# Index keys split two steps ahead, a deeper queue of selection rounds, value pages V3 before the cross pages, and a fourth raw weight buffer

## The chip, the cores and the metric

The kernel runs on one core of one Trainium2 chip. The metric is the time of one execution on the device, in microseconds (us). A core has TensorE (PE) for matmuls, with its weight loads shown apart as PEld, VectorE (DVE), ScalarE (ACT), GpSimd (POOL) and SyncE (SP), which here issues the transfers. Each engine works through its own list of instructions in order; where two engines share data, one waits for the other by a semaphore.

## The reference

One step of a decoder layer, for a prompt of 256 tokens and 8 sample requests with 8 new tokens each (320 token rows, `NT`), model width 2048. One projection of the residual stream feeds three branches: sparse attention (A) whose keys are chosen by an indexer, a gated linear recurrence (B), and cross-attention to a memory (M). Each branch is multiplied by a SiLU gate, the three are concatenated and go through an output projection and a layer norm.

```python
def _in_proj(h, w, pos):
    z = jnp.einsum('btd,dn->btn', h, w)
    aq, ak, av, ag, iq, ik, iw, bq, bf, bi, bg, mq, mg = jnp.split(z, cuts, axis=-1)
    ...
def _indexer_scores(iq, iw, ik):
    dots = jnp.einsum('bthd,bld->bthl', iq, ik) * (D_IDX ** -0.5)          # 16 heads x 64
    return jnp.einsum('bth,bthl->btl', iw * (H_IDX ** -0.5), relu(dots))
def _dsa_sample(q, k_new, v_new, iq, iw, ik_new, cache_k, cache_v, cache_idx_k, page_table):
    ik_all = concatenate([cache_idx_k[page_table], ik_new])                # 2048 + 8 keys a request
    sc = where(kpos <= qpos, _indexer_scores(iq, iw, ik_all), -inf)
    _, sel = lax.top_k(sc, 256)
    # attention of 8 heads x 128 over the 256 selected keys and values of the paged cache
    ...
def _merge(...):
    cat = concatenate([a * silu(ag), rmsnorm(b) * silu(bg), m * silu(mg)])  # 2048 wide
    return layernorm(ALPHA * h + cat @ w_out)
```

## The kernel before

**Precision.** All matmuls against weights are done in three products of a fast fp32 form (fp32r): each operand is split into a high part and a rest. For the residual stream these are `xh` and `xl`; for a weight half (128 x 512 of a raw weight tile `wr`, 128 x 1024) ACT casts `wh` from `wr` and DVE or POOL subtracts `wl = wr - wh`. There are three buffers of `wr` and four each of `wh` and `wl`. The first 52 weights have their `wl` on DVE; later ones go to DVE or POOL, whichever is free sooner by the planner's costs (`TT`). While the selection on the sample scores runs, `hold_dve` adds 4 us to DVE's side of that choice.

**Stages.** PE works through the list `PROJECTIONS`: index keys and queries, attention queries, keys and values, the recurrence's inputs, gates, then 16 weights of kind "mem" (the projection of the memory), then the rest and last the output projection `wo`. One 128-deep slice of a projection is three matmuls `pj<-xh,wh`, `pj<-xl,wh`, `pj<-xh,wl` of 320 columns. `xh` and `xl` are reused for the concatenated branches (`cat`) when the last projection has read them: process `split` casts `xh<-cat` on ACT and subtracts `xl` on POOL and DVE, and the first `wo` matmul (`mA<-wh,xh`) needs them.

**Pages.** Between projection slices PE makes visits to the cache pages, which SP loads into six buffers `pg`: keys (`kv<-pg,qpad`, 32 or 16 matmuls) and values (`va<-pg,PT`). `PAGES` is their order: K0 to K3 and V0 to V3 are pairs of heads of the paged cache, 8 units each, XK and XV the cross-attention cache.

**Indexer on the samples.** `idx_sample` has 20 steps, 16 of 512 keys and 4 of the 8 new keys. A step's keys are gathered, then split by `stack(k)`: ACT casts the high halves and DVE subtracts the two rests into the tile `cat1`, in one of two slots by the parity of the step (64x512 each, rows `cat<-pg,cat` and `cat<-S,cat` on DVE; in the order below the tile's name is `cat_4_84` before and `cat_5_83` after). Four matmuls `mA<-cat,bp` or `mB<-cat,bp` follow, then relu, and every few steps the sums over heads (`va<-cat,t`). `topk_sample` then takes 32 rounds of MAX8 and MATCH_REPLACE8 over the scores on DVE (tile `PT`). `idx_prompt` does the same for the prompt, in smaller rounds (tile `cat0`), and leaves its mask in `pbias`. `attn_scores` and `attn_values` are the prompt's attention, and `"attn" in done` marks their end.

**What sets the order.** The program is a planner: class `Plan` keeps a time for each engine from cost formulas, `plan.now` follows PE, and the loop at the end of the function emits loads (`loads`), weight splits (`prep`), evacuations of finished projections and pieces of the background processes (generators) whenever their conditions are met at the planned time. `need(...)` makes a process wait until its operands are planned to be ready, `idle("DVE", x)` until DVE's planned queue is at most x us, and `calm()` holds the recurrence's long rows back while an engine's queue is over `CALM` = 4 us. The result is a fixed list of instructions for every engine. All instructions that go through the planner's `Engine` carry one line of the profile, L154, so they are told apart by their tiles. `tabm` is the rope table of the attention heads, `lbt` the lower bounds of the recurrence.

Of the kernel before, what the change touches and what calls it, by code (L numbers as in the profile page):

```python
# [26 lines left out]
NS, NT = 64, 320  # L27
PAST = 2048
HALF = 1032
PROJECTIONS = ["ikw", "iq", "aq", "ak", "av", "b0", "b1", "g0", "b2", "g1", "b3", "mem", "mq", "g3", "g2"]  # L30
PAGES = ["K0", "K1", "V0", "K2", "V1", "V2", "K3", "XK0", "XK1", "XV0", "XV1", "V3"]
DEFER = (0,)
MIX = [(1, 2), (1, 4), (1, 6), (2, 0)]
KORDER = (0, 2, 4, 6, 12, 14, 8, 10)
# [10 lines left out]
CALM = 4.0  # L45
# [180 lines left out]
def hymba_step(ctx: ExitStack, tc: tile.TileContext, I, O):  # L226
    nc = tc.nc
    plan = Plan()
# [39 lines left out]
    def const(shape, name, dt=F32):  # L268
        return pool.tile(shape, dt, name=name, tag=name, bufs=1)
# [42 lines left out]
    xh = const([128, 16, NT], "xh", F32R)  # L312
    xl = const([128, 16, NT], "xl", F32R)
    ident = const([128, 128], "ident")
    tabm = const([128, 2, NT], "tabm")
    csm = const([128, 297], "csm")
    cu8 = const([128, 304], "cu8", U8)
    ptab = const([1, 128], "ptab", I32)
# [7 lines left out]
    one = const([128, 1], "one")  # L326
    onesm = const([128, 128], "onesm")
    emat = const([128, 2, 2, 2, 128], "emat", BF)
    pbias = const([128, 384], "pbias")
    maskb = const([128, HALF], "maskb", BF)  # L330
    early, stacked = new([128, 2880], "cat0"), new([128, 2240], "cat1", F32R)
    plan.split |= {early.tensor.name, stacked.tensor.name}
# [13 lines left out]
    done = set()  # L346
# [232 lines left out]

    WR, WH, WL = {}, {}, {}  # L580

    def load_w(i):
        s = wspec[i]
        WR[i] = s["home"] if "home" in s else new([128, 1024], "wr")
        SP.dma_start(WR[i][:, 0:s["n"]], s["src"])
        if s["kind"] == "mem":
            s["raw"] = T(256)
            SP.dma_start(s["raw"], I["memT"][:, s["k"], :])
# [259 lines left out]
    def idx_sample():  # L848
# [67 lines left out]

        while not keys_in(0):
            yield
        kk = stack(0)
        rs, full = {}, None  # L920
        for k, (sp, c, f, a) in enumerate(steps):
            n = kk[0].shape[-1]
            yield need(ql, qh, *kk, ps=2, lag=LAG2)
            pd = [PS([128, 512]), PS([128, 512])]
            for j in range(2):
                b = 4 * sp + 2 * a + j
                PE.matmul(pd[j][:, 0:n], qh[:, b], kk[j], start=True, stop=False)
                PE.matmul(pd[j][:, 0:n], qlr[:, b], kk[j], start=False, stop=True)
            if full:
                sums(*full)  # L930
                full = None
            r = rs.setdefault((c, f), [])
            for j in range(2):
                r.append(relu_slot(n))
                if j == 0 or plan.t["ACT"] < plan.t["DVE"] + 0.5:
                    ACT.activation(r[-1], pd[j][:, 0:n], AF.Relu)
                else:
                    DVE.tensor_scalar(r[-1], pd[j][:, 0:n], 0.0, None, op0=OP.max)
            if a == 1 and (c, f) in ((0, 0), (2, 1)):
                full, rs = (sp, rs), {}  # L940
            while not keys_in(k + 1):
                yield
            if k + 1 < len(steps):
                kk = stack(k + 1)
                yield
        yield need(*[x for r in full[1].values() for x in r], ps=1)
        sums(*full)
# [6 lines left out]
    def topk_sample(sc, arena):  # L954
        w1 = arena[:, HALF:2 * HALF]
        L = arena[:, 2 * HALF:2 * HALF + 256]
        for r in range(32):
            yield from idle("DVE", 0.3)
            m8 = L[:, 8 * r:8 * r + 8]
            src = sc if r == 0 else w1  # L960
            DVE.max(m8, src)
            DVE.match_replace(out=w1, in_to_replace=m8, in_values=src, imm_value=FLOOR)
# [283 lines left out]

    def calm():

        while max(plan.t[e] for e in ("DVE", "POOL", "ACT")) > plan.now + CALM:
            yield  # L1250

    def hgrn():
# [648 lines left out]
    def loads():  # L1901
        nonlocal nw, npg
        while True:
            if plan.t["SP"] > plan.now + 0.5:
                return
            if nw < len(wspec) and wspec[nw].get("ref"):
                nw += 1
                continue
            if nw < len(wspec) and nw < half + 5 and plan.slot_free("wr", 3) <= plan.now + 1 and nw - nprep < 3 \
                    and (wspec[nw]["kind"] != "mem" or has_room(3)):  # L1910
                load_w(nw)
                nw += 1
                continue
            if outq and plan.avail(outq[0][1]) <= plan.now:
                dst, src = outq.pop(0)
                SP.dma_start(dst, src)
                free(src)
                continue
            if later_in and plan.t["DMA"] < plan.now + IDLE:
                dst, src = later_in.pop(0)  # L1920
                SP.dma_start(dst, src)
                continue
            n, b = divmod(npg, 2)
            if (half > 46 and n < len(punits) and len(PG) + ("q" in st) + ("more" in st) + ci_live(0) < BUFS["pg"] and n <= nunit + 2
                    and plan.slot_free("pg", BUFS["pg"]) <= plan.now + 0.2 and plan.t["DMA"] < plan.now + 8):
                load_pages(n, b)
                npg += 1
                continue
            if ("soft", 3) in done and half > n_in - 6 and ("r", 1) not in st:
                ln_load(0)  # L1930
                ln_load(1)
                continue
            if n == len(punits) and nunit == n and half > n_in - 6 and ("r", 2) not in st:
                ln_load(2)
                continue
            return
# [177 lines left out]
```

## Time and profile before

| | |
|---|---|
| median of 3 runs | 877.13 us (876.77 to 878.39) |
| profiled execution, own time | 878.17 us |
| its span | 876.4 us |
| granted TensorE clock | 0.998 |
| PE, DVE, ACT, POOL busy | 860.5, 558.0, 423.0, 311.7 us |
| last matmul starts | 868.17 us |
| moved by DMA | 266.55 MB, 304 GB/s in the mean |

The profile is of one execution. Times within it run from the start of the span; the runs' times also hold what lies around the span. "Idle before" in a row is the time for which the engine did nothing ahead of it, with what ended the wait. The ends of matmuls are modelled: a 320-column matmul shows 0.31 us, while the next one starts 0.15 us later.

### The profile page before, as it was taken

Reading aid. Unit: us, or ns where it says so; the run is one execution under the profiler, and the core shown is the slowest. Engines: PE = TensorE matmul, PEld = TensorE weight load, DVE = VectorE, ACT = ScalarE, POOL = GpSimd, SP = SyncE. Lnnn points to the kernel's source line nnn. Section 1 sums busy time; section 2 is a strip of 40 time slices with the busy share of each in tenths; the row PEclk is TensorE's granted clock in tenths of the full one; section 3 lists DMA queues with packets and bytes.
Section 4 is the critical chain, followed back from the end, with each engine's and each line's share of the span. In section 5 each row is a group of like instructions: output and inputs, shape, how many; then the busy total and the mean of one; then the engine's idle time right before and its main releaser. Section 6 shows DMA issues by size and latency. Waiting matters only on the chain.

```text
span 876.4 us, 19974 instructions
## 1 busy us (share of the span) xinstructions
PE 860.5 (98%) x6972; PEld 730.7 (83%) x6974; DVE 558.0 (64%) x1128; ACT 423.0 (48%) x909; POOL 311.7 (36%) x310
## 2 busy tenths in 40 slices
PE   9999999999999999999999999999999999999996
PEld 8999898878988998879888786777888878788885
DVE  6778989748789984645745563585444333943655
ACT  6445666545463444435545364444444433744432
POOL 0543562255644461322433142334222000613424
PEclk9999999999999999999999999999999999999999
DMA  8555544899999975999999999999998999876633
GB/s 309 182 165 160 158 144 146 300 342 405 362 410 337 372 260 161 339 411 354 398 367 399 412 377 401 405 347 383 325 408 331 350 384 384 295 269 200 192 101 120
DMA packets 84375, 266.55 MB, mean 304 GB/s; under 512 B 10609, under 2 KB 21810, under 8 KB 83634
## 3 DMA queue, kind: packets, MB, share of 16 engines
q1 hardware_dynamic: 83250, 263.18, 81.3%
q0 software_dynamic: 1024, 2.10, 0.8%
q8 instruction: 55, 0.90, 0.4%
q14 instruction: 46, 0.38, 0.1%
HBM read 256.50 MB, written 8.73 MB: 303 GB/s over the span
## 4 chain that ended last, share of the span: by engine, by line
PE 91%; DMA 3%; DVE 2%; ACT 1%; SPq 1%; issue 1%; DVEq 0%; ACTq 0%
PE pj L154 53%; PE mB L154 11%; PE va L154 10%; PE mA L154 9%; PE kv L154 7%; DMA pg<-in_ck 2%; SPq L154 1%; ACT wh L154 1%; DVE wl L154 1%; DMA pg<-in_xT 1%; DVE t L154 1%; DMA wr<-in_wt 0%; DVE pg L154 0%; ACT t L154 0%; DVE cat L154 0%
## 5 line engine op out<-in xcount | busy, mean ns | idle before, releaser
L154 PE MATMUL pj<-xh,wh 128*128 128x320 f32 x1008 | 321.9, 319 | 0.0
L154 PE MATMUL pj<-xh,wl 128*128 128x320 f32 x1008 | 311.5, 309 | 0.0
L154 PE MATMUL pj<-xl,wh 128*128 128x320 f32 x1008 | 311.3, 309 | 0.0
L154 ACT CAST wh<-wr 128x512 fp32r<-128x512 f32 x338 | 205.4, 618 | 210.9 <-PE pj L154 155.3
L154 DVE TENSOR_TENSOR wl<-wr,wh 128x512 fp32r<-128x512 f32 x231 | 178.2, 785 | 183.1 <-ACT wh L154 180.2
L154 POOL TENSOR_TENSOR wl<-wr,wh 128x512 fp32r<-128x512 f32 x107 | 145.2, 1362 | 296.8 <-ACT wh L154 272.9
L154 PEld LDWEIGHTS pj<-xh,wh 128*128 128x128 f32 x1008 | 189.4, 188 | 18.4 <-issue 12.7
L154 PEld LDWEIGHTS pj<-xl,wh 128*128 128x128 f32 x1008 | 189.5, 188 | 1.3
L154 PEld LDWEIGHTS pj<-xh,wl 128*128 128x128 f32 x1008 | 189.2, 188 | 0.0
L154 POOL TENSOR_TENSOR t<-t,t 128x320 f32<-128x320 f32 (+3 forms) x44 | 41.1, 935 | 88.5 <-DVE t L154 41.2
L154 PE MATMUL kv<-pg,qpad 128*32 128x256 f32 x1032 | 62.7, 380 | 3.4 <-DMA pg<-in_ck 3.4
L154 PE MATMUL va<-pg,PT 128*32 128x512 f32 x512 | 59.6, 596 | 0.0
L154 PEld LDWEIGHTS kv<-pg,qpad 128*32 128x32 f32 x1032 | 33.4, 110 | 27.2 <-issue 5.7
L154 PEld LDWEIGHTS va<-pg,PT 128*32 128x32 f32 x512 | 15.1, 109 | 30.5 <-issue 29.3
L154 DVE MAX8 PT<-PT 128x8 f32<-128x1032 f32 x32 | 39.5, 1234 | 0.5
L154 DVE MATCH_REPLACE8 PT<-PT 128x1032 f32<-128x1032 f32 x32 | 39.0, 1217 | 0.0
L154 ACT ACTIVATE t<-t 128x320 f32<-128x320 f32 (+1 forms) x44 | 18.5, 455 | 24.7 <-DVE t L154 24.4
L154 POOL TENSOR_TENSOR t<-t,tabm 128x320 f32<-128x320 f32 x16 | 14.0, 878 | 39.1 <-DVE t L154 35.4
L154 POOL DMA_INDIRECT pg<-in_ci,row x16 | 16.6, 1040 | 26.8 <-DVE row L154 19.9
L154 DVE TENSOR_TENSOR t<-t,t 128x320 f32<-128x320 f32 (+4 forms) x28 | 17.6, 629 | 13.4 <-ACT t L154 6.9
L154 ACT ACTIVATE S<-kv 128x512 f32<-128x512 f32 x16 | 9.6, 598 | 32.6 <-PE kv L154 32.6
L154 PE MATMUL mB<-t,wh 128*128 128x256 f32 x128 | 24.0, 286 | 0.0
(360 smaller groups left out, 1314.1 us busy)
## 6 DMA issues: line engine op xcount, KB each, us to landing
pg<-in_ck SPq DMA_DIRECT2D x128, 512.0 KB
pg<-in_cv SPq DMA_DIRECT2D x128, 512.0 KB
wr<-in_wt SPq DMA_DIRECT2D x126, 512.0 KB
wr<-in_wo SPq DMA_DIRECT2D x36, 512.0 KB
wr<-in_wm SPq DMA_DIRECT2D x16, 512.0 KB
pg<-in_cXK SPq DMA_DIRECT2D x8, 512.0 KB
pg<-in_cXV SPq DMA_DIRECT2D x8, 512.0 KB
pg<-in_xT SPq DMA_DIRECT2D x8, 320.0 KB
```

What stands on the lines that cost most here:

```text
L154: res = f(*a, **k)
```

## The change

It has five parts. In `PAGES` the last value pages V3 come directly behind K3, ahead of the cross pages. The rope table `tabm` (640 columns) and `pbias` (384) become one tile `tp` of the size of a raw weight, and when the prompt's attention is done that tile serves as a fourth raw weight buffer: `wr_free`, `tp_free` and `raws_in` say when one may be loaded. In `idx_sample` the keys are split two steps ahead (list `ahead`), once DVE's planned queue is at most 2.2 us. In `topk_sample` a round is issued when DVE's queue is at most 1.0 us, not 0.3. In `calm` the limit is 1.0 us, not 4.0, while the next weight is of kind "mem".

```diff
-PAGES = ["K0", "K1", "V0", "K2", "V1", "V2", "K3", "XK0", "XK1", "XV0", "XV1", "V3"]
+PAGES = ["K0", "K1", "V0", "K2", "V1", "V2", "K3", "V3", "XK0", "XK1", "XV0", "XV1"]
...
-    tabm = const([128, 2, NT], "tabm")
+    tp = new([128, 1024], "tp")
+    plan.split.add(tp.tensor.name)
+    tabm = tp[:, 0:640].rearrange("p (a b) -> p a b", a=2)
...
-    pbias = const([128, 384], "pbias")
+    pbias = tp[:, 640:1024]
...
+    def raws_in(tp):
+        return sum(not wspec[i].get("ref") and bool(wspec[i].get("tp")) == tp for i in range(nprep, nw))
+    def wr_free():
+        return raws_in(False) < 3 and plan.slot_free("wr", 3) <= plan.now + 1
+    def tp_free():
+        return "attn" in done and not raws_in(True) and plan.slot_free("tp", 1) <= plan.now + 1
     def load_w(i):
         s = wspec[i]
-        WR[i] = s["home"] if "home" in s else new([128, 1024], "wr")
+        WR[i] = s["home"] if "home" in s else new([128, 1024], "wr" if "attn" not in done or wr_free() else "tp")
+        s["tp"] = WR[i].tensor.name.startswith("tp")
...
         while not keys_in(0):
             yield
-        kk = stack(0)
+        ahead = [stack(0)]
+        while not keys_in(1):
+            yield
+        yield from idle("DVE", 2.2)
+        ahead.append(stack(1))
         rs, full = {}, None
         for k, (sp, c, f, a) in enumerate(steps):
+            kk = ahead.pop(0)
...
-            while not keys_in(k + 1):
+            while not keys_in(k + 2):
                 yield
-            if k + 1 < len(steps):
-                kk = stack(k + 1)
+            if k + 2 < len(steps):
+                yield from idle("DVE", 2.2)
+                ahead.append(stack(k + 2))
                 yield
...
         for r in range(32):
-            yield from idle("DVE", 0.3)
+            yield from idle("DVE", 1.0)
...
-        while max(plan.t[e] for e in ("DVE", "POOL", "ACT")) > plan.now + CALM:
+        while max(plan.t[e] for e in ("DVE", "POOL", "ACT")) > plan.now + (1.0 if half < len(wspec) and wspec[half]["kind"] == "mem" else CALM):
...
-            if nw < len(wspec) and nw < half + 5 and plan.slot_free("wr", 3) <= plan.now + 1 and nw - nprep < 3 \
+            if nw < len(wspec) and nw < half + 5 and (wr_free() or tp_free()) \
```

Since the planner follows its costs, the whole order behind the first changed decision moves. Three places show it. A row gives the instruction's number on its engine, the operation, the tile written and the tiles read, and the shape.

The first is DVE in the index stage. Before, each pair of key splits (`cat_4_84`, two splits of 64x512) has several weight splits between it and the next:

```order
149 L154 TENSOR_TENSOR cat_4_84<-pg_395,cat_4_84 64x512 x2
150 L154 TENSOR_TENSOR wl_1657<-wr_1428,wh_1656 128x512
151 L154 STREAM_SHUFFLE t_1677<-pj_1532 128x320
152 L154 TENSOR_TENSOR t_1678<-pj_1532,tabm 128x320
153 L154 TENSOR_TENSOR wl_1694<-wr_1522,wh_1693 128x512
154 L154 TENSOR_TENSOR cat_4_84<-S_396,cat_4_84 64x512 x2
155 L154 CAST row_1725<-rows 128x2
156 L154 TENSOR_TENSOR wl_1746<-wr_1522,wh_1745 128x512
157 L154 TENSOR_TENSOR wl_1774<-wr_1586,wh_1773 128x512
```

After, from the same place (`cat_5_83`):

```order
149 L154 TENSOR_TENSOR cat_5_83<-pg_394,cat_5_83 64x512 x2
150 L154 TENSOR_TENSOR wl_1658<-wr_1427,wh_1657 128x512
151 L154 STREAM_SHUFFLE t_1671<-pj_1513 128x320
152 L154 TENSOR_TENSOR t_1672<-pj_1513,tp_66 128x320
153 L154 TENSOR_TENSOR cat_5_83<-S_395,cat_5_83 64x512 x2
154 L154 TENSOR_TENSOR wl_1707<-wr_1520,wh_1706 128x512
155 L154 CAST row_1724<-rows 128x2
156 L154 TENSOR_TENSOR wl_1745<-wr_1520,wh_1744 128x512
157 L154 TENSOR_TENSOR cat_5_83<-pg_394,cat_5_83 64x512 x2
158 L154 TENSOR_TENSOR wl_1777<-wr_1587,wh_1776 128x512
159 L154 TENSOR_TENSOR cat_5_83<-S_395,cat_5_83 64x512 x2
```

Four pairs of key splits now stand where two stood. From the first pair to the last, DVE had 40 weight splits between them and has 23.

The second is PE at the change from the projections to `wo`. Before, V3's last units (`va<-pg,PT`) stand between the last projection matmul and the first `wo` matmul:

```order
4207 L154 MATMUL pj_11940<-xh,wl_11937 128x320
4208 L154 MATMUL va_11414<-pg_11721,PT_10875 32x512 x2
4209 L154 MATMUL va_11414<-pg_11770,PT_10875 32x512 x2
4210 L154 MATMUL va_11414<-pg_11721,PT_10875 32x512 x2
4211 L154 MATMUL va_11414<-pg_11770,PT_10875 32x512 x2
4212 L154 MATMUL va_11414<-pg_11866,PT_10875 32x512 x2
4213 L154 MATMUL va_11414<-pg_11893,PT_10875 32x512 x2
4214 L154 MATMUL va_11414<-pg_11866,PT_10875 32x512 x2
4215 L154 MATMUL va_11414<-pg_11893,PT_10875 32x512 x2
4216 L154 MATMUL va_11414<-avS,PT_10875 32x512 x4
4217 L154 MATMUL mA_12070<-wh_11957,xh 128x512
4218 L154 MATMUL mA_12070<-wh_11957,xl 128x512
```

After, the first `wo` matmul follows at once:

```order
4216 L154 MATMUL pj_11982<-xh,wh_11978 128x320
4217 L154 MATMUL pj_11982<-xl,wh_11978 128x320
4218 L154 MATMUL pj_11982<-xh,wl_11979 128x320
4219 L154 MATMUL mA_12079<-wh_11997,xh 128x512
4220 L154 MATMUL mA_12079<-wh_11997,xl 128x512
```

V3's units have moved ahead of the cross pages' visits, into the projections.

The third is SP where the first "mem" weight (`in_wm`) is loaded. Before, value pages (`in_cv`, V2's) follow it:

```order
847 L154 DMA pg_8447<-in_cv 128x1024
848 L154 TENSOR_LOAD ptab
849 L154 ISA x3
850 L154 DMA pg_8447<-in_cv 128x1024
851 L154 DMA wr_8484<-in_wm 128x1024
852 L154 DMA t_8486<-in_memT 128x256
853 L154 TENSOR_LOAD ptab
854 L154 ISA x3
855 L154 DMA pg_8510<-in_cv 128x1024
```

After, it goes into the tile `tp`, and key pages of K3 (`in_ck`) follow:

```order
919 L154 DMA pg_8761<-in_cv 128x1024
920 L154 TENSOR_LOAD ptab
921 L154 ISA x3
922 L154 DMA pg_8761<-in_cv 128x1024
923 L154 DMA tp_8814<-in_wm 128x1024
924 L154 DMA t_8816<-in_memT 128x256
925 L154 TENSOR_LOAD ptab
926 L154 ISA x3
927 L154 DMA pg_8839<-in_ck 128x1024
```

All of V2 has been loaded ahead of the first "mem" weight.

## The prediction

> **What bounds the kernel now.** The page comes first: busy shares, slices and the chain that ended last.
>
> ```profile
> PE 860.5 (98%) x6972; PEld 730.7 (83%) x6974; DVE 558.0 (64%) x1128; ACT 423.0 (48%) x909; POOL 311.7 (36%) x310
> PE   9999999999999999999999999999999999999996
> DVE  6778989748789984645745563585444333943655
> GB/s 309 182 165 160 158 144 146 300 342 405 362 410 337 372 260 161 339 411 354 398 367 399 412 377 401 405 347 383 325 408 331 350 384 384 295 269 200 192 101 120
> PE 91%; DMA 3%; DVE 2%; ACT 1%; SPq 1%; issue 1%; DVEq 0%; ACTq 0%
> ```
>
> PE is busy in every slice but the last and carries 91% of the chain. The same matmuls run after the change, so only three things can move the time: PE's waits, its turns from one kind of matmul to another, and the eight microseconds behind the last matmul, which the change leaves alone. The waits of PE, in the list of waits, are therefore the whole stake:
>
> ```profile
> PE kv L154 <- DMA pg<-in_ck: 3.4, 4, 1.6
> PE pj L154 <- issue: 1.4, 1, 1.4
> ...
> PE mA L154 <- DVE cat L154: 0.5, 2, 0.3
> PE mA L154 <- ACT PT L154: 0.4, 1, 0.4
> ...
> PE mB L154 <- DVE t L154: 0.3, 1, 0.3
> ```
>
> The columns are total, times and longest. The first row is key pages of K3 that arrive late in the memory-projection stage, the second a pause in a row of such matmuls, the others operands of single steps. The rest of the list belongs to the first 13 us. Next I read the windows, for the resource that comes behind PE in each stage:
>
> ```profile
> 84.40:146.00 61.60, 60.87 (x399) 54.45 (x399) 56.48 (x134) 40.75 (x80) 30.20 (x33) 1.00 0.50 150
> 280.00:340.00 60.00, 59.98 (x498) 55.11 (x497) 52.16 (x77) 28.18 (x56) 29.32 (x20) 1.00 0.78 281
> 330.00:528.00 198.00, 197.84 (x1863) 162.74 (x1866) 107.64 (x224) 94.88 (x201) 58.60 (x69) 1.00 0.94 361
> 541.00:637.00 96.00, 90.92 (x872) 71.30 (x870) 57.65 (x115) 46.65 (x116) 35.05 (x38) 1.00 0.98 368
> ```
>
> Behind the window's length stand the busy times of PE, PEld, DVE, ACT and POOL, the clock, the DMA share and the rate. In the index stage (84 to 146) DVE is busy 56.48 of 61.60 us, with the DMA half idle. In the stage with the late pages (541 to 637) the DMA engines are full, and before it, at 280 to 340, they had stood idle for 22%.
>
> **The change part by part. Value pages V3 ahead of the cross pages, and the fourth raw buffer: the late pages go.** In the new order the whole of V2 is read before the memory projection begins, and that stage holds K3 alone; masks and scores come earlier, so that pages are asked for in the idle stretch. If its 22% is used, 0.22 x 60 us = 13 us of transfer are done early. The pages of K3 were late by 3.4 us in sum, 1.6 us at most, so I take all four waits away: -3.4 us. The bounds are 0 (the hole isn't filled) and -3.4.
>
> What is late next is the projection stage: with the same pages pulled forward it has to bring some 76.5 MB (counted from the loads in the new order between the same matmuls) in the 198 us in which 361 GB/s moved at a share of 0.94. A full queue would give 361 / 0.94 = 384 GB/s, so 199.2 us: late by 1.2 us; by the 541 to 637 row, 368 / 0.98 = 375 GB/s, 203.7 us, late by 5.7 us; by the best slices of the page (405, 410, 412) not late at all. I take +1.0 (0 to 5.7), because single slices show that the queue can exceed its mean when asked.
>
> The Trainium skill, page "SBUF — State Buffer", section "A bandwidth-pool intuition that's wrong (but worth ruling out)", puts the path from HBM to one core at about 358 GB/s; by that figure the 76.5 MB would take an estimated 213.7 us, 15.7 more than the stage has, and the kernel would end near 889 us. The trace goes against it as a ceiling, since slices stand at 405, 410 and 412 GB/s and the whole busy stage at 361 with 6% idle.
>
> **V3's cover at the end of the projections: lost.** At the change to the output stage the timeline shows:
>
> ```profile
> 746.05 0.31 PE L154 MATMUL pj<-xh,wl 128*128 128x320 f32 x1
> 746.25 0.62 ACT L154 CAST wh<-wr 128x512 fp32r<-128x512 f32 x1 [1.14 <-PE pj L154]
> 746.29 3.64 PE L154 MATMUL va<-pg,PT 128*32 128x512 f32 x32
> 746.78 1.63 ACT L154 CAST xh<-cat 128x256 fp32r<-128x256 f32 x5
> 747.25 2.69 POOL L154 TENSOR_TENSOR xl<-cat,xh 128x256 fp32r<-128x256 f32 x3 [30.69 <-ACT xh L154]
> 749.75 1.04 PE L154 MATMUL va<-avS,PT 128*32 128x512 f32 x8
> 750.72 0.50 PE L154 MATMUL mA<-wh,xh 128*128 128x512 f32 x1
> ```
>
> xh and xl hold the split residual stream and may be rewritten for the concatenated branches only after the last projection matmul (746.05). ACT then casts a weight (it needs the buffer of that same matmul), starts xh at 746.78, and POOL begins the first xl at 747.25 and needs 2.69 / 3 = 0.90 us, to 748.15. Under this lie V3's last two visits, 746.29 to 750.7. In the new order nothing lies there: the first wo matmul follows the last projection matmul. It can take xh, 0.23 us of work, and the second needs xl at 748.2. So PE stands 748.2 - 0.23 - 746.2 = +1.8 us (1.4 if ACT's two casts change places, 2.7 if a second xl is waited for). The visits themselves aren't lost, they are done earlier.
>
> **Index keys two steps ahead: the steps come closer.** Before, 16 wide and 4 narrow index steps are spread from 85.7 to 187; after, all stand within 84 slices of the projection, which with PE's own work (84 x 3 matmuls of 0.147, 16 steps of 0.93, 4 of 0.5, three summing visits of 1.9) end about 144. Each wide step costs DVE two key splits. The DVE groups of this stretch, with shapes apart, and its waits:
>
> ```profile
> L154 DVE TENSOR_TENSOR wl<-wr,wh 128x512 fp32r<-128x512 f32 x28 | 21.5, 786 | 0.3
> L154 DVE TENSOR_TENSOR cat<-S,cat 64x512 fp32r<-64x512 f32 x10 | 7.9, 786 | 3.4 <-ACT cat L154 3.2
> L154 DVE TENSOR_TENSOR cat<-pg,cat 64x512 fp32r<-64x512 f32 x10 | 7.1, 712 | 0.5 <-ACT cat L154 0.2
> L154 DVE STREAM_SHUFFLE t<-pj 128x320 f32<-128x320 f32 x7 | 3.6, 521 | 0.0
> L154 DVE TENSOR_TENSOR t<-pj,tabm 128x320 f32<-128x320 f32 x7 | 3.3, 476 | 0.0
> ```
>
> From the first key split to the last, the new order gives DVE 23 weight splits, 32 key splits, 12 selection rounds on the prompt, 5 rope pairs and small work. With the row means: 23 x 0.786 + 32 x 0.75 = 42.1; rope 5 x 1.0 = 5.0; the rest (rounds at 0.66 to 0.92, masks, casts, adds) 19, in all 66 us. The rows overlap: the 21 groups of that view sum to 61.7 us where DVE was busy 56.48, so the true cost is 66 x 56.48 / 61.7 = 60.5 us. DVE has from 84.4 to 144, 59.6 us, and no wait may remain. Two steps of lead should remove the waits on ACT (3.6 us here) only in part; with half left, 60.5 + 1.8 = 62.3 us, 2.7 short. Weight splits stand up to one quarter weight (12 matmuls, 1.8 us) ahead of PE, but the lb chain and the next rounds come right behind. I take +2.5 us of PE waits (0 if the lead covers it, 6.4 if the row means hold). Against it stand the two waits on DVE cat and the one on ACT PT, which go: -0.9.
>
> **Deeper queue of selection rounds.** One round on the sample scores is:
>
> ```profile
> 192.99 1.23 DVE L154 MAX8 PT<-PT 128x8 f32<-128x1032 f32 x1
> 194.25 0.09 DVE L154 MATCH_VALUE_LOAD PT<-PT 128x8 f32 x1
> 194.33 1.22 DVE L154 MATCH_REPLACE8 PT<-PT 128x1032 f32<-128x1032 f32 x1
> ```
>
> That is 2.5 us of DVE in one piece; up to 1.0 us of queue may now stand ahead of it, not 0.3. Whoever needs DVE behind it waits 0.7 us longer at most: weight splits (now shared with POOL) and rope. The splits are ahead by 1.8 us, which hides it; without that cover each of the 32 rounds could cost 0.7. I take 0 (0 to +2). **Earlier loads before a memory weight (the calm margin)** shift HGRN work; its visits may find an operand late, as mB did for DVE t (0.3): -0.3 goes and +0.3 comes, bounds +-1.
>
> **What else.** A matmul row lasts 0.31 us while the next starts 0.15 later, so a wait is hidden by some 0.16 us in the list: eight waits gone, -1.3. The pause of 1.4 us on "issue" depends on where the code lies; with a chance near 0.6 that one returns, -0.6. Turns:
>
> ```profile
> 587.20 0.28 PE L154 MATMUL mB<-t,wl 128*128 128x256 f32 x1
> 587.41 1.93 PE L154 MATMUL kv<-pg,qpad 128*32 128x256 f32 x32
> 589.27 0.74 PE L154 MATMUL pj<-wh,t 128*128 128x512 f32 x2
> 589.85 0.40 PE L154 MATMUL pj<-wl,t 128*128 128x512 f32 x1
> ```
>
> The visit begins 0.21 behind a matmul of 0.12, and the first 512-wide pair behind it takes 0.58 where two take 0.46: some 0.2 us a visit. The new order has 3 visits of 128x32 fewer and 9 turns to full fp32 fewer (62 to 53): 12 x 0.1 to 0.2, -1.5 (0 to -2.4).
>
> The sum: -3.4 + 1.0 + 1.8 + 2.5 - 0.9 + 0 - 0.3 + 0.3 - 1.3 - 0.6 - 1.5 = -2.4 us. The profiled run took 878.17 us (span 876.4); it becomes about 875.8. The median of the runs shown, 877.13, lies 1.0 lower: **874.7 us**.
>
> **The rivals.** First, slower: DVE becomes the bound from 84 to 190. The place is the index stage, and the point is where key splits, weight splits and prompt rounds exceed 59.6 us by more than the lead of 1.8. At the row means (66 us) it is 6.4 short, the weight splits behind it another 2, so PE stands 8 us in place of 2.5: 880. For it: busy 56.48 of 61.60 already, and 12 key splits more in the stretch. Against it: 5 weight splits fewer there, and overlap of rows. The same page of the Trainium skill, section "Who interferes with whom", has a DVE instruction with two SBUF inputs shut out a POOL instruction that reads SBUF and be shut out by it; with 30 us of POOL in the window that speaks for the dearer rows. A split that met nothing, from the timeline, against the mean of 786 above, agrees with it:
>
> ```profile
> 117.23 0.69 DVE L154 TENSOR_TENSOR wl<-wr,wh 128x512 fp32r<-128x512 f32 x1
> ```
>
> Second, the bandwidth: the projection stage asks for 386 GB/s, and pages come late in V1 to V2 visits. With 375 GB/s the waits are 5.7 us, not 1.0: 879.4. Against it, the slices above 400.
>
> Third, nothing measurable: the page waits only move (0 for -3.4) and the turns are worth nothing, but DVE's wait is small: 874.7 + 3.4 + 1.5 - 2.5 = 877.1.
>
> Fourth, better: DVE's lead covers all (0 for 2.5), the DMA keeps up (0 for 1.0): 871.2.
>
> **How the numbers follow.** A measurement of this kernel can tell about 0.2%, 1.75 us, from no change. My forecast (872.5 to 875.4 with its near variants) has 0.37, the better case 0.13, nothing measurable 0.24, DVE as the bound 0.15, bandwidth 0.11. Faster: 0.50; within 0.2%: 0.25 (a sliver of the DVE and bandwidth cases ends there, as a sliver of the third doesn't); slower: 0.25. The range leaves out a tenth on each side: 870 to 881.
>
> **What would show it.** In the changed profile: no PE wait on pg<-in_ck above 0.5 us in the memory stage; the hole at 280 to 340 gone from the GB/s slices; a PE wait of 1.4 to 2 us at the first wo matmul, on POOL's xl or ACT's xh; the last index step at 146 to 151 with PE waits on DVE cat or wl of 1.5 to 6 us before 190. I am wrong if DVE keeps pace with no waits (then about 872), if page waits reappear between 330 and 530 (879 or more), or if the wait at the first wo matmul is absent.

## The result, and the profile after

The changed kernel takes 882.50 us (median of 4 runs, 881.87 to 882.73) against 876.98 us of the kernel before: a ratio of 1.0061, with a 95% interval of 1.0047 to 1.0075. It is 5.5 us slower; the forecast was 2.4 us faster. The profiled execution took 882.36 us, its span is 880.6 us, 4.2 us over that of before, and the granted clock is 0.995 in the mean, not 0.998.

The page of the changed kernel, where the lines shown of before stood:

```profile
PE 861.9 (98%) x6974; PEld 730.9 (83%) x6974; DVE 560.9 (64%) x1136; ACT 422.5 (48%) x913; POOL 296.7 (34%) x298
PE   9999999999999999999999999998999999999996
GB/s 305 185 163 160 160 118 100 220 414 365 396 385 363 384 406 388 409 365 410 345 385 404 350 392 405 403 407 287 390 311 387 402 252 263 248 183 184 197 97 120
PE 83%; DMA 4%; DVE 3%; issue 2%; ACT 1%; POOL 1%; SPq 0%; DVEq 0%; POOLq 0%; ACTq 0%
```

The hole in the transfers at 280 to 340 us is gone, as forecast (260 and 161 GB/s have become 406 and 388). PE's share of the chain has gone from 91% to 83%. The list of PE's waits, in the order of before (total, times, longest):

```profile
PE pj L154 <- DVE t L154: 3.4, 1, 3.4
PE kv L154 <- DMA bp<-in_st: 1.7, 1, 1.7
...
PE mB L154 <- ACT t L154: 1.0, 1, 1.0
PE mA L154 <- ACT xh L154: 0.9, 1, 0.9
PE mA L154 <- DVE cat L154: 0.5, 2, 0.3
PE mA L154 <- POOL xl L154: 0.5, 1, 0.5
...
PE mB L154 <- DVE cat L154: 0.3, 1, 0.3
```

The four waits on K3's pages and the pause on "issue" at 543 us are gone. In their place stand one wait of 3.4 us in the same memory stage, 1.7 us in a visit to key pages at 409 us (the releaser that the list names, the recurrence's state, is no operand of that matmul), 1.0 us at 631 us, and two waits at the first `wo` matmul. The windows show the stages:

```profile
84.40:146.00 61.60, 60.56 (x370) 48.69 (x369) 59.22 (x134) 50.71 (x101) 28.21 (x29) 1.00 0.41 125
330.00:528.00 198.00, 196.31 (x1850) 159.95 (x1852) 100.37 (x191) 85.14 (x185) 45.78 (x53) 1.00 0.99 383
541.00:637.00 96.00, 91.60 (x913) 74.90 (x913) 59.11 (x109) 46.45 (x107) 33.57 (x37) 0.98 0.98 375
604.00:608.00 4.00, 1.46 (x4) 1.17 (x5) 4.00 (x6) 0.00 (x0) 2.21 (x3) 0.75 0.10 36
608.00:612.00 4.00, 4.00 (x22) 3.55 (x21) 2.61 (x7) 1.91 (x4) 1.68 (x2) 0.82 0.92 255
```

In the index stage DVE is busy 59.22 of 61.60 us, yet PE stands for only about one. The projections ask for 383 GB/s at a share of 0.99: the queue is full. In the memory stage the clock, the third figure from the end, falls to 0.75 and 0.82 around 606 us.

**The 1.7 us at 409 is no late page.** In the trace no transfer of data is completed in the 1.4 us ahead of its end. What lands, at 407.69, is a packet of 16 KB on the queue that brings an engine's instructions:

```profile
q8 instruction: 55, 0.90, 0.4%
```

Fifty-five packets for PE's 14081 instructions are 256 instructions each. PE goes on 1.6 us behind the packet, at number 6851 of its list as the trace has it, which is 26 x 256 + 195. The pause on "issue" of before is of the same kind: its packet landed at 541.42, PE went on at 542.67, at number 9408 = 36 x 256 + 192. Over all the kernels of this document there are 20 such stops of more than 0.4 us; each one lies 192 to 195 instructions behind a multiple of 256 and ends 1.25 to 1.6 us behind such a packet. So I read them as waits for PE's own instructions. Why a packet came late at these places and in time at most others is open.

**The 3.4 us at 606.** The timeline of the three engines that prepare operands, ahead of the matmul `pj<-wh,t` that waits (the `t` of 128x256 is the rest of the split memory, `ml`):

```profile
597.18 0.60 ACT L154 ACTIVATE S<-kv 128x512 f32<-128x512 f32 x1 [4.59 <-PE kv L154]
600.55 0.47 ACT L154 ACTIVATE t<-t 128x320 f32<-128x320 f32 x1 [1.44 <-DVE t L154]
600.79 2.15 DVE L154 RECIPROCAL t<-t 128x320 f32<-128x320 f32 x1
600.93 0.60 ACT L154 CAST wh<-wr 128x512 fp32r<-128x512 f32 x1
603.55 1.00 POOL L154 TENSOR_TENSOR bp<-t,t 128x320 f32<-128x320 f32 x1 [3.94 <-DVE t L154]
603.74 1.35 DVE L154 TENSOR_TENSOR wl<-wr,wh 128x512 fp32r<-128x512 f32 x1
604.81 1.40 POOL L154 TENSOR_TENSOR wl<-tp,wh 128x512 fp32r<-128x512 f32 x1
605.01 1.48 DVE L154 TENSOR_TENSOR t<-t,t 128x256 fp32r<-128x256 f32 x1
606.41 0.68 DVE L154 TENSOR_TENSOR wl<-wr,wh 128x512 fp32r<-128x512 f32 x1
606.54 0.80 PE L154 MATMUL pj<-wh,t 128*128 128x512 f32 x1 [3.37 <-DVE t L154]
607.01 0.41 DVE L154 TENSOR_TENSOR t<-t,t 128x256 fp32r<-128x256 f32 x1
607.14 0.63 PE L154 MATMUL pj<-wl,t 128*128 128x512 f32 x1
```

ACT stood 4.59 us behind the exponential of the key scores, whose visit PE had not done, and 1.44 us more, to 600.55, behind a row of the recurrence on DVE; the casts of the weight that is late stand behind both in its list. When they came, DVE had the recurrence's second reciprocal (2.15 us, with its neighbours 2.95 us to 603.74) ahead of their rests. Then two splits took 1.35 and 1.48 us while POOL ran; the same two forms took 0.68 and 0.41 us a moment later, when POOL stood still. That is an estimated 1.7 us of the 3.4 (0.67 + 1.07).

**The clock behind it.** The first `pj` matmuls behind the wait start 0.43 to 0.60 us apart, where 0.23 is usual: from 606.54 to 609.46 PE does 1.5 us of work in 2.9. So 1.4 us more are lost with every matmul busy.

**The sum.** The idle times ahead of PE's rows in the trace, by stage (worked out from all of them; ends of matmuls are modelled, so some 0.16 us of each wait are not in it):

| PE idle, us | first 30 us | index, to 180 | projections, to 530 | memory, to 645 | to 742 | wo | sum |
|---|---|---|---|---|---|---|---|
| before | 1.6 | 0.9 | 0.2 | 5.1 | 0.2 | 0.0 | 7.9 |
| after | 1.9 | 1.2 | 1.8 | 4.4 | 0.0 | 1.4 | 10.7 |

10.7 - 7.9 = 2.8 us, and 1.4 us of slow clock, make the 4.2 us of the spans.

### The profile page after: what moved, and what is told of

Same layout as the page of the kernel before. It is cut to its first block, busy times and chain, and to the rows that moved or that the text cites. A ratio compares the mean times of both kernels' runs of the same rounds, so it can differ in the third digit from the quotient of the medians.

```text
span 880.6 us, 20011 instructions
## 1 busy us (share of the span) xinstructions
PE 861.9 (98%) x6974; PEld 730.9 (83%) x6974; DVE 560.9 (64%) x1136; ACT 422.5 (48%) x913; POOL 296.7 (34%) x298
## 4 chain that ended last, share of the span: by engine, by line
PE 83%; DMA 4%; DVE 3%; issue 2%; ACT 1%; POOL 1%; SPq 0%; DVEq 0%; POOLq 0%; ACTq 0%
PE pj L154 48%; PE mB L154 11%; PE va L154 9%; PE mA L154 8%; PE kv L154 7%; DMA wr<-in_wm 2%; DVE cat L154 1%; DVE wl L154 1%; DMA pg<-in_ck 1%; DMA bp<-in_st 1%; ACT cat L154 1%; ACT wh L154 1%; DMA wr<-in_wt 0%; DVE pg L154 0%; DVE t L154 0%
## 5 line engine op out<-in xcount | busy, mean ns | idle before, releaser
L154 DVE TENSOR_TENSOR wl<-wr,wh 128x512 fp32r<-128x512 f32 x208 | 158.0, 771 | 184.6 <-ACT wh L154 176.0
L154 ACT CAST wh<-wr 128x512 fp32r<-128x512 f32 x294 | 178.5, 618 | 174.4 <-PE pj L154 147.4
L154 POOL TENSOR_TENSOR wl<-wr,wh 128x512 fp32r<-128x512 f32 x86 | 115.2, 1348 | 239.9 <-ACT wh L154 198.8
L154 POOL TENSOR_TENSOR t<-t,t 128x320 f32<-128x320 f32 (+3 forms) x41 | 38.2, 933 | 106.6 <-DVE t L154 43.7
L154 PE MATMUL kv<-pg,qpad 128*32 128x256 f32 x1032 | 60.7, 380 | 1.7 <-DMA bp<-in_st 1.7
L154 DVE TENSOR_TENSOR wl<-tp,wh 128x512 fp32r<-128x512 f32 x32 | 25.8, 809 | 28.2 <-ACT wh L154 28.0
L154 ACT CAST wh<-tp 128x512 fp32r<-128x512 f32 x44 | 26.7, 618 | 24.8 <-PE pj L154 21.6
L154 POOL TENSOR_TENSOR wl<-tp,wh 128x512 fp32r<-128x512 f32 x12 | 16.1, 1342 | 57.4 <-DVE t L154 29.4
L154 DVE TENSOR_TENSOR t<-t,t 128x320 f32<-128x320 f32 (+4 forms) x31 | 20.7, 667 | 13.7 <-POOL t L154 10.5
L154 POOL TENSOR_TENSOR t<-t,tp 128x320 f32<-128x320 f32 x16 | 14.1, 881 | 45.3 <-DVE t L154 44.2
```

The costliest lines, as they stand in the source:

```text
L154: res = f(*a, **k)
```

## The experiments

Ratios are of medians, to the kernel before on the same chip (876.6 to 877.4 us), with 95% intervals; the profiles are of one execution each. Each kernel is planned anew, so a part that is taken out also moves what stands behind it.

### One part taken out of the changed kernel

V3 back behind the cross pages:

```diff
-PAGES = [..., "K3", "V3", "XK0", "XK1", "XV0", "XV1"]
+PAGES = [..., "K3", "XK0", "XK1", "XV0", "XV1", "V3"]
```

> The changed kernel with V3 put back behind the cross pages, all other parts kept. Theory A (the loss is local: 3.4 us at one operand of the memory projection with a lower clock behind it, 1.7 us of late pages at 409, 1.0 us at 631, 1.8 us at the first wo matmul): only the 1.8 us at the first wo matmul go, since V3's visits cover it again; the wait in the memory stage stays at 3 to 3.5 us: 880.5 to 881 us. Rival B (the order of the pages brings the whole loss, by the transfers): back to about 877 us, with no wait over 2 us in the memory stage.

Measured 884.02 us, ratio 1.0078 (1.0061 to 1.0095). The wait at 606 stays at 3.4 us, and PE's idle time in `wo` falls from 1.4 to 0.03 us, both as theory A has it. Its time, 880.5 to 881 us, was missed by 3 us: 1.1 us of a new wait at 698 came, and more that is not visible as waits, so that nothing was gained. Rival B falls.

The recurrence's margin at 4.0 us throughout:

```diff
-... > plan.now + (1.0 if half < len(wspec) and wspec[half]["kind"] == "mem" else CALM):
+... > plan.now + CALM:
```

> The changed kernel with the recurrence's queue margin back at 4.0 us in the memory stage. Theory A (the recurrence's DVE rows stand ahead of the memory weight's splits because ACT and DVE fell behind there, not because of the margin; the DVE list around the second reciprocal is the same with either margin): 3.4 us at the same operand again, 882 to 883 us. Rival C (the smaller margin itself moved the rows there): the wait is under 1 us and the time 878 to 879.5 us.

Measured 884.59 us, 1.0097 (1.0076 to 1.0117). The 3.4 us stay as theory A had it (its 882 to 883 us were too low), and the wait at 631 grows from 1.0 to 2.2 us. The margin isn't what put the rows there; the smaller one helps.

Keys one step ahead (`ahead` and its 2.2 us gates taken out, `keys_in(k + 1)`):

> The changed kernel with index keys split one step ahead again. Theory A: the waits of PE on key splits between 100 and 145 us (1.4 us in four places, with what matmul rows hide) shrink to those of before (0.7); the memory stage's list is another, so the 3.4 us stay or go by chance: 876 to 882 us, and whatever it is shows as the memory stage's waits, not as index waits. Rival D (DVE in the index stage is the bound and the loss starts there): 877 us with index waits gone and the memory stage's waits unchanged.

Measured 876.90 us, 1.0000 (0.9990 to 1.0009): all 5.5 us are back. The waits on key splits between 80 and 190 us go, but they were 0.6 us; the memory stage's idle time falls from 4.4 to 2.3 us, the projections' from 1.8 to 0, and the clock stays full. So this part brings the loss, but for nine tenths not at the place where its work is: rival D, whose time was met, falls by the place, and theory A's "by chance" isn't yet an explanation.

The selection rounds at a queue of 0.3 us again (`idle("DVE", 1.0)` to `0.3`), and then three raw buffers (`tp_free` returns False):

> The changed kernel with the selection rounds let in at a DVE queue of 0.3 us again. Its DVE list has no memory operand split behind the second reciprocal of the memory stage. Theory A: no wait over 1.5 us there, the waits at the first wo matmul (1.4 to 2.4 us) and in the index stage (1.4 us) stay: 877 to 879 us. Rival F (the deeper queue has no part in the loss): 882 us.

> The changed kernel with three raw weight buffers (the shared tile is never used for weights). Its DVE list has two score rows and no memory operand right behind the second reciprocal. Theory A: no 3.4 us wait at that operand, 877.5 to 880 us. Rival G (the fourth buffer is neutral): 882 us with the 3.4 us wait.

With 0.3 us: 879.54 us, 1.0031 (1.0019 to 1.0042), no wait over 1 us in the memory stage, 2.3 us idle in `wo`. Theory A's waits were met, its time (877 to 879 us) missed by 0.5 us, and rival F falls: in the changed kernel the deeper queue costs 3.0 us. With three buffers: 883.58 us, 1.0066 (1.0049 to 1.0083). The wait at that operand is another one, of 1.6 us, with one of 0.5 us and a slow clock behind; 1.5 us are a stop for instructions at 410, and the splits of a `wo` weight come 1.5 us late. Theory A's time was missed; rival G is right that the buffer is neutral here, though by other waits than it named.

### The wait at 606 by itself

The recurrence starts no head in the memory stage:

```diff
+            while half < len(wspec) and wspec[half]["kind"] == "mem":
+                yield
             yield need(f, bi)
             vN = new([128, 3, 128], "vN")
```

> The changed kernel in which the recurrence begins no new head (transposes, the two reciprocals and what follows on DVE) while the next weight is one of the memory projection; the matmuls and the work are the same. Theory A (3.4 us at 606 is the recurrence's 3.3 us of DVE rows, the second reciprocal among them, that stand ahead of the memory operand's split, and the lower clock behind it is a consequence): the 3.4 us wait is gone, the clock stays at 1.00 in that stage, and 4 to 5.5 us come back: 877 to 878.5 us. Rival E (the weight lands late behind pages in full DMA queues, and DVE's rows only fill the time): the wait stays at 2 us or more, 880 us or more.

Measured 885.90 us, 1.0103 (1.0086 to 1.0120). The wait at 606 is gone, and PE is busy without a break there at full clock; so the recurrence's rows were part of its cause (the rest of the order moved with them). But the time isn't back: one wait of 3.4 us on value pages ends at 666, with the clock at half behind it (first window 604 to 608, then 666 to 670):

```profile
604.00:608.00 4.00, 4.00 (x28) 3.65 (x27) 1.92 (x3) 2.12 (x5) 1.89 (x2) 1.00 0.96 332
666.00:668.00 2.00, 1.78 (x10) 0.36 (x12) 0.78 (x2) 0.81 (x3) 0.90 (x1) 0.67 1.03 422
668.00:670.00 2.00, 2.00 (x6) 0.65 (x3) 0.00 (x0) 0.00 (x0) 1.00 (x1) 0.50 1.01 410
```

The DMA share there is 1.0. Theory A missed the time by 7 us; rival E's (880 us or more) was met, but not its place, for this wait is on value pages and not on a weight.

The first selection round held until weight 50 (`while half < 50: yield` ahead of the rounds):

> The changed kernel with the first selection round on the sample scores held back until weight 50, so that the rounds begin near 188 us, as with a queue of 0.3 us, and not at 157 us; rounds then go at a queue of 1.0 us. Theory A (the losses are places in the order: the recurrence's second reciprocal ahead of a memory operand): its list still has that operand behind the reciprocal, the 3.4 us wait stays, 881 to 883 us. Rival H (selection rounds between 157 and 188 us are what costs: they push page reads early, and the transfers trail from then on): no page wait at 409, no 3.4 us wait, 878.5 to 880 us.

Measured 883.30 us, 1.0071 (1.0054 to 1.0088). The 3.4 us at 607 stay, the stop for instructions at 410 shrinks to 0.7 us, and 1.5 us on `maskb` at 298 come in its place. Early rounds aren't what costs: rival H falls, and theory A's time was missed by 0.3 us.

The second reciprocal taken off DVE, in the changed kernel:

```diff
-            DVE.tensor_scalar(kk, kk, 1.0, None, op0=OP.add)
-            DVE.reciprocal(kk, kk)
+            ACT.activation(kk, kk, AF.Ln, bias=one[:, 0:1])
+            ACT.activation(kk, kk, AF.Exp, scale=-1.0)
```

> The changed kernel with the recurrence's second reciprocal (one add and one reciprocal on DVE, 0.32 + 2.15 us a head) replaced by a logarithm and an exponential on ACT (0.47 each); the value is the same function. Theory A (those DVE rows ahead of the memory operand's split are the wait): no wait over 1.5 us in the memory stage, no half-speed clock, 876.5 to 879 us. Rival I (keys two steps ahead bring the order into a stage where something is always late, and another operand takes the place): a wait of 2 us or more between 540 and 700 us, 881 us or more.

Measured 882.98 us, 1.0069 (1.0047 to 1.0091). The wait at that operand is 2.25 us, not 3.37, and one of 1.95 us on "issue" comes at 558, a stop for instructions (number 9664 of PE's list, 37 x 256 + 192): rival I's time is met, though the new wait is not for an operand. What is left at the operand is shown by the timeline:

```profile
608.99 1.01 POOL L154 TENSOR_TENSOR bp<-t,t 128x320 f32<-128x320 f32 x1 [2.98 <-DVE t L154]
609.19 1.35 DVE L154 TENSOR_TENSOR wl<-wr,wh 128x512 fp32r<-128x512 f32 x1
610.47 1.48 DVE L154 TENSOR_TENSOR t<-t,t 128x256 fp32r<-128x256 f32 x1
611.88 0.68 DVE L154 TENSOR_TENSOR wl<-wr,wh 128x512 fp32r<-128x512 f32 x1
612.01 0.79 PE L154 MATMUL pj<-wh,t 128*128 128x512 f32 x1 [2.25 <-DVE t L154]
612.48 0.41 DVE L154 TENSOR_TENSOR t<-t,t 128x256 fp32r<-128x256 f32 x1
```

The same pair again takes 1.35 and 1.48 us beside POOL, 0.68 and 0.41 without it. The reciprocal was worth 1.1 us of the wait; the collision is worth an estimated 1.7, which no run takes away by itself.

### One or two parts added to the kernel before

V3 ahead of the cross pages alone, keys two steps ahead alone, selection rounds at 1.0 us alone, and these last two together (edits as in the change):

> The kernel before with V3 put ahead of the cross pages and nothing else. Theory A: everything up to the memory projection as before, and one new wait of 1.8 us (0.9 to 1.1 on xh, 0.5 to 0.8 on xl) at the first wo matmul, 878.8 us. Rival: the wait is met by something earlier in that order (visits moved, fewer turns), 877 us.

> The kernel before with keys two steps ahead and nothing else. Theory A: waits on key splits between 100 and 145 us of 1.0 to 1.5 us, the rest in the manner of the run with all but the deeper queue (879.5 less the 2.3 us at the first wo matmul): 876.5 to 878 us. Rival D (DVE is the bound in the index stage): 880 us or more.

> The kernel before with selection rounds let in at a DVE queue of 1.0 us and nothing else. Theory A: selection ends near 289 us, not 301, the late pages of K3 (3.4 us) and the pause of 1.4 us go, and this part alone is what makes the version with keys one step ahead and V3 last faster: 873.5 to 875.5 us. Rival: that gain belongs to the fourth buffer or the margin, 877 us.

> The kernel before with only two parts: keys two steps ahead and selection rounds at a queue of 1.0 us. If these two bring the loss: selection ends near 274 us, a page wait near 409 us, 880 to 884 us, as slow as with all five parts. If V3, the buffer or the margin bring it: 875 to 878 us.

V3 alone: 876.48 us, 0.9996 (0.9986 to 1.0006), no wait at the first `wo` matmul, as the rival had it: there the cross values' visit falls between the last projection matmul and `wo` and covers it. The lines are PE's:

```profile
744.98 0.31 PE L154 MATMUL pj<-xh,wl 128*128 128x320 f32 x1
745.22 1.92 PE L154 MATMUL va<-pg,t 128*32 128x512 f32 x16
```

Keys alone: 882.83 us, 1.0061 (1.0044 to 1.0077). Selection alone: 881.99 us, 1.0055 (1.0039 to 1.0072). Both: 889.01 us, 1.0141 (1.0121 to 1.0160). For the first two I had expected 876.5 to 878 and 873.5 to 875.5, for both together 880 to 884: three misses. Rival D's time was met for the keys, not its place: PE's idle time in the index stage is 1.8 us, in the memory stage 5.4, in `wo` 1.9. With the selection alone the index stage has 0.9, the memory stage 5.8, `wo` 1.9. Each of these two parts, by itself, moves work so that a visit in the memory stage stands 2.3 or 2.5 us within itself. The profile calls it "issue", and it is the stop for instructions again: it ends 1.3 and 1.4 us behind a packet, at 192 or 193 behind a multiple of 256 in PE's list. With the keys alone two more such stops, of 0.6 and 0.7 us, come at 473 and 543. So, in the profiled executions, 2.2 of the 5.2 us by which the keys alone lengthen the span, and 1.1 of the 3.2 us for the selection alone, are such stops beyond the 1.4 us of before.

V3 alone leaves the hole in the transfers at 307 to 351 us (292 and 145 GB/s) and 2.0 us of late K3 pages. With the keys or the selection alone no K3 page is late, and the deeper slice of the hole rises from 161 to 330 and 336 GB/s.

### The fastest version, and what it owes to which part

Keys one step ahead and V3 last, so that the buffer, the queue of 1.0 us and the margin of 1.0 us are left:

> The changed kernel with keys one step ahead and V3 behind the cross pages, so that only the fourth weight buffer, the deeper selection queue and the margin are left. Theory A: as with keys one step ahead alone, no wait over 1 us before 640, and V3 covers the first wo matmul (2.4 us of waits on xh and xl there go): 874.5 us, the fastest version. Rival: the visits of V3 at the end meet late operands of their own, 876.5 us or more.

Measured 874.56 us, 0.9971 (0.9960 to 0.9983): faster than both kernels, as theory A had it. Among its longest waits behind the first 30 us are these, and V3 covers the change to `wo`:

```profile
PE mA L154 <- DVE cat L154: 1.0, 2, 0.7
PE mA L154 <- ACT t L154: 0.5, 1, 0.5
...
741.81 3.64 PE L154 MATMUL va<-pg,PT 128*32 128x512 f32 x32
745.27 1.04 PE L154 MATMUL va<-avS,PT 128*32 128x512 f32 x8
746.24 0.50 PE L154 MATMUL mA<-wh,xh 128*128 128x512 f32 x1
```

PE's idle time is 4.4 us in all: 1.4 in the memory stage and none in `wo`. With V3 early (keys one step ahead, above) it was 876.90 us with 2.4 us idle in `wo`. From this version one part each was changed: the reciprocal on ACT, three buffers, the margin at 4.0 us:

> The fastest version so far (keys one step ahead, V3 last, fourth buffer, deeper queue, margin: 874.6 us) with the second reciprocal on ACT. Its matmuls wait for 1.4 us in the memory stage. Theory A: at most those 1.4 us go, 873 to 874.5 us. Rival I: the order changes and new waits come, 875.5 us or more.

> The fastest version with three raw weight buffers. If the fourth buffer is what separates it from the deeper queue alone (882.0): 880 to 883 us with 4 us or more of waits in the memory stage. If the margin is: 874 to 876 us.

> The fastest version with the recurrence's margin at 4.0 us throughout. If the margin is what separates it from the deeper queue alone: 879 to 883 us. If the buffer is: 874 to 876 us.

875.82 us, 0.9985 (0.9975 to 0.9994); 878.76 us, 1.0022 (1.0012 to 1.0031); 883.19 us, 1.0071 (1.0054 to 1.0088). So taking 2.5 us a head off DVE brings nothing there (a wait of 1.1 us at 691 comes, and rival I's time is met), the buffer is worth half a per cent and the margin one per cent. The time with three buffers lies between the two ranges that I had given; with the margin at 4.0 us it is 0.2 us above the range for the margin. There PE waits 1.1 us on ACT S and 2.0 us on DVE PT at 645 to 649, again with a slow clock: ACT's exponential over the scores takes 2.06 us, and a weight split of 1.35 us stands ahead of DVE's copy of PT. No row of the recurrence stands between them, so how the margin leads there is not shown.

## Why the prediction was wrong

The sign is wrong, and the range missed the time by 1.5 us. Step by step:

- **Late pages go, -3.4 us.** They went, and the hole at 280 to 340 us was filled. But the step credits V3's place and the buffer. V3 alone leaves 2.0 us of them, and without the buffer (the fastest version with three) none is late; with the keys alone or the deeper queue alone, whose last selection rounds begin at 286 and 288 us, not at 300, they go.
- **What is late next, +1.0.** The projection stage does ask for 383 GB/s at a share of 0.99, and no wait on a page stands there: the lower bound of 0 came true. The 1.7 us at 409 are a wait for instructions. The step looked for the next late thing among transfers alone; in the memory stage, where the pages had been late, it was an operand of DVE.
- **Earlier loads before a memory weight (-0.3 + 0.3, bounds +-1).** This is the term that failed. In its place stand 3.4 us on the memory's rest, 1.0 us at 631 and 1.4 us of slow clock: 5.8 us where the bounds were one either way. I had priced what the margin does to that stage and not what the other parts do to it: an operand chain over ACT and DVE with the recurrence's rows in the middle. The margin is not what brought it (with 4.0 us the wait stays). The keys and the deeper queue are: without either of them no wait over 1 us stands in that stage, and 5.5 or 3.0 us come back. The late pages of before were not what had covered this chain: 2.3 of their 3.4 us (at 613.67 and 637.05) lie behind the last matmul of the memory at 607.75, and with keys one step ahead no page is late, yet no wait in that stage is longer than 0.6 us.
- **V3's cover at the end of the projections, +1.8 us.** The timeline says 1.0 us ahead of the first `wo` matmul and 0.8 ahead of the second, 1.8 in sum (1.4 of them visible as waits). Right in the place, the engines and the size. The runs add that the cover may be another visit: with V3 alone moved, cross values lay there and nothing was lost.
- **Keys two steps ahead, +2.5 us with -0.9 for waits that go.** Over-priced at its place: PE's idle time in the index stage went from 0.9 to 1.2 us, with DVE busy 59.22 of 61.60 us. DVE was nearly as full as worked out (60.5 us were expected); the two steps of lead absorbed it. Under-priced as a part: the runs give it +0.6% alone, +0.6% in the changed kernel and about +1.1% in the fastest version (884.02 against 874.56 us, ratios 1.0078 and 0.9971), most of it spent in later stages.
- **Deeper queue of rounds, 0 (0 to +2).** Alone it costs 0.55% and in the changed kernel 3.0 us, both beyond the bound. With the buffer and the margin it is part of a version that is 0.3% faster. I priced it by the rounds and their neighbours on DVE, and it moves the end of the selection (the last round begins at 288 us alone and at 273 in the changed kernel, not at 300). That it costs by this is not shown.
- **Hidden shares, turns and the pause, -1.3 - 1.5 - 0.6.** The pause depended on where the code lies, as the step says, and it returned: 1.7 us at 409 for 1.4 us at 543. The other two did not show in the sum: visible waits and the clock already make the measured 4.2 us. Whether new waits hid as much as was gained was not measured apart.

The slower rival had the right sign for the wrong reason: it put DVE's overload into the index stage. The collision of DVE and POOL that I counted for it was real, but it cost where both had work for one operand. That the keys part costs time, and for the most part behind its own stage, is shown by four pairs of runs (with and without it in the kernel before, with the selection alone, in the changed kernel and in the fastest version); which single decision of the order does it isn't. With the reciprocal off DVE or the recurrence held out, the 3.4 us shrink or go and as much comes elsewhere, and in the kernel with keys and selection alone 3.6 us are left that neither visible waits nor the clock explain (its idle time is 4.8 us over that of before, its span 8.4). That stays open.

## What to carry to other kernels

Before you book a wait that goes as a gain, list for the same stage, in the new order, what stands ahead of each operand's last producer, and price the chain that has the least left over, on the engine queues that are in order (here ACT behind a score activation, DVE behind a reciprocal). Find the place of a pause on "issue" in the engine's own list before you call it a late transfer. Where a planner sets the order, price a part by its stages downstream too, and test parts alone and in pairs: two parts that cost 0.6% each made 1.4% together, and one of them was part of the best version with two others. Work that stands between the last use of a buffer and the first use of its new contents is worth its length only as long as something lies there; what lies there doesn't matter.

## What the runs showed of the hardware that was not expected

A wait of 3.4 us on PE cost nearly 5, since the granted clock fell to 0.50 shortly before its end and came back some 3 us later; at the wait to 666, in the run without a head in the memory stage, the means were 0.67 and 0.50 for two microseconds each. The length of the wait alone does not decide it: a single wait of 2.5 us, to 621.3, left the clock at 1.00 in the kernel with the selection alone:

```profile
622.00:624.00 2.00, 2.00 (x17) 1.68 (x12) 0.38 (x2) 1.04 (x4) 0.00 (x0) 1.00 1.01 396
```

In the changed kernel with three buffers, two waits of 1.6 and 0.5 us, to 602.4 and 603.4, with one matmul between them, brought it to 0.50:

```profile
604.00:606.00 2.00, 2.00 (x8) 1.71 (x7) 1.38 (x3) 0.79 (x3) 1.03 (x2) 0.50 0.79 213
```

The clock's own record in the traces settles how. In eight kernels it fell once before the last matmul, each time for one stretch of 3.41 us (606.00 to 609.41 in the changed kernel). From its begin to the begin of the slow clock at the program's end it is a whole number of such stretches in all eight (79 x 3.413 us in the changed kernel). So the time is cut into windows of 3.41 us that do not start with a wait. In the window ahead of the slow one PE had stood idle for 2.8 us in the changed kernel, 2.1 us with three buffers, and 2.0 to 3.0 us in all eight. In the kernel with the selection alone the wait of 2.5 us is shared by two windows, at most 1.8 us in one; no window from 20 us on, in a kernel whose clock stayed, holds more than 2.0 us. So here the limit is near 2.0 us of 3.41, by the visible waits (1.99 us lowered the clock in one kernel, 2.00 us did not in another).

The Trainium skill, page "TensorE: Matmul & The Clock Gate", section "What's actually happening", says that the clock is halved after an idle window of about 3.4 us and released after a busy one, and that the windows run freely. The length, the free run and the half at 0.50 agree with it; that a window with up to 1.4 us of work in it lowers the clock does not follow from that sentence.

PE also stops at fixed places of its own list: all 20 pauses of more than 0.4 us that no operand explains, over the kernels of this document, stand 192 to 195 instructions behind a multiple of 256, and end 1.25 to 1.6 us behind a 16 KB packet of the instruction queue. They cost 0.4 to 2.5 us each, so part of the price of any change to this kernel is which work such a place falls on.

A split on DVE of two SBUF inputs takes 0.68 or 0.41 us alone and 1.35 or 1.48 us beside a POOL instruction of 1.0 to 1.4 us, in two kernels alike. The same skill, page "SBUF — State Buffer", section "Who interferes with whom", says that such a DVE instruction and a GpSimd instruction that reads SBUF contend for one read port; the trace agrees, with both forms shown with and without POOL at work within a few microseconds.
